# One decoder layer on one Trainium2 core: three weight tiles instead of four beside the time mixing, its tiles in two pools, and nine modulation steps at the second norm

## The chip, the cores and the metric

One core of one Trainium2 chip runs the whole kernel as one launch. The metric is the device time of that launch in microseconds. The chip has five engines that matter here: TensorE (PE, with its weight loads shown apart as PEld), VectorE (DVE), ScalarE (ACT), GpSimd (POOL) and SyncE (SP), which here only issues DMAs.

## The reference

One inference step of one layer on 256 prompt tokens and 8 sequences of 4 sample tokens, so 288 columns (NT) of width 2048, in float32. Cut to what matters:

```python
mod = silu(c) @ ada_w + ada_b                 # 2048 -> 6 vectors of 2048
sh1, sc1, ga1, sh2, sc2, ga2 = split(mod, 6)
h = rmsnorm(x, g0) * (1 + sc1) + sh1
proj = h @ w_in                               # 2048 x 6144: r, k, v and three conv inputs
w, a, g = small low-rank products of h
y, S = wkv7_scan(state, r, w, k, v, kk, kk*a) # 16 heads of 64, delta rule, token by token
o_rwkv = (groupnorm(y) + bonus) * g
o_conv = bg * causal_conv3(cg * hc)
x = x + ga1 * (concat(o_rwkv, o_conv) @ w_out)
h2 = rmsnorm(x, g1) * (1 + sc2) + sh2
ua, ub = split(causal_conv3(h2 @ ffn_up), 2)  # 2048 x 11264
x = x + ga2 * ((silu(ua) * ub) @ ffn_down)    # 5632 x 2048
return rmsnorm(x, final_g), and the new states
```

## The kernel before

Activations lie with the features on the partitions and the 288 columns in the free dimension. Every large product runs in three passes over a reduced float format: `load_piece` (L168) brings a piece of 1 MB of weights into a tile of the ring `rawtile` (L137); `split` (L149) makes of each half of it a rounded copy `whi` (ACT, the cast of L154) and a remainder `wlo` (DVE, L156) in a buffer of the pool `hl`; `mm3` (L163) issues three matmuls of 288 columns for each 128x128 block (`actH`x`whi`, `actL`x`whi`, `actH`x`wlo`, L164 to L166). A half piece is 24 matmuls. The ring has 3 tiles that stay for the whole kernel and some more that `work_pools` (L96) opens for a part: 2 in the first part, 1 beside the decay products and the conv, 0 in the second part, 1 from the output projection on. `hl` has 3 buffers.

The six modulation vectors come from `ada_vector` (L247), a generator whose every step loads 1 MB of `ada_w` into a ring tile and issues four side by side matmuls into a bank named `ada` (printed at L298 and L301, the lines of the helper that issues them). Sixteen steps make a vector. The generator `rest` has the 64 steps of GA1, SC2, SH2 and GA2; each `step(rest)` in the program puts one step among other work, and PE order is chosen by a scheduler that goes by the order of the program, by what is ready and by pools.

The stages, in the order of the span:

- 0 to 42 us set-up and first norm, 42 to 270 us the first three blocks of `w_in` and the low-rank products.
- 270 to 415 us the conv stage. For each of the 8 pairs of heads p: `first(p)`, `blocks_of(p-1)` (64x64 and 32x32 matmuls at L635 and L637 whose results go out as `dN` and `dNs`, L641 and L642), two pieces of the conv's `w_in`, two modulation steps (L725). A period takes 17 us. SP issues the four loads and the small stores in one queue, and a load that waits for its tile holds up whatever stands behind it.
- 415 to 475 us: `substitute` (L644 to L669) inverts 32x32 triangles on DVE and POOL (L664, L665), ACT copies the result (`TL`, L666) and stores it as `dT` and `dTT`, while TensorE drains the rest of the conv.
- 475 to 698 us: `second(p)` eight times, some 25 to 30 us each, chains of small matmuls with DVE and ACT between them. `T1` and `TTc` come back from `dT` and `dTT` through SP (L994 to L998). Three modulation steps stand ahead of it, five behind each p, seven behind the last (L1003). Its tiles lie in one pool, `tm2`.
- 700 to 805 us: the output projection `w_out` through `gemm2` (L1063), 8 double columns with the upper half of the inputs first, so that the conv's half starts it. `turn_out` (L1085) transposes rows of states that go out.
- 805 to 817 us: `taps` (transposes of the conv state of the feed forward, L1044), three modulation steps, the sum over partitions by a matmul with ones (L1120), `rms_scale` (L1025 to L1031, a Newton step on DVE behind exp and ln on ACT), then `make_h2` (L1128 to L1132).
- 817 to 1640 us: `up(g)` and `down(g)` for 11 groups of 4 blocks of the feed forward; then the last norm and the rows `yo` that go out.

## Time and profile before

| | us |
|---|---|
| median of 3 runs | 1698.98 (1683.72 to 1699.15) |
| the profiled execution | 1694.01 |
| its span | 1692.2 |
| mean granted clock of TensorE | 0.983 of full speed |
| PE busy | 1630.8 |
| DVE busy | 1160.7 |
| ACT busy | 713.6 |
| POOL busy | 387.1 |

The page counts busy time in the span; the profiled execution's own time is 1.8 us longer than its span. A row of the timeline ends in a bracket where the engine was idle ahead of it: the idle time, and what released it. `xcount` merges neighbouring instructions. In the view by stretches the column of PEclk is the granted clock of TensorE, 1.00 for 2.4 GHz and 0.5 for 1.2 GHz, so a value between them is a stretch with both. Lines (L154) are lines of the kernel before; in the kernel after the change the same statement has another number.

### The profile page before, as it was taken

The page shows a single profiled execution, that of the slowest core. Times are in us where ns is not written, and L with a number is a line of the kernel's source. Part 1 is how long each engine was busy: PE and PEld are TensorE (multiplying, and loading weights), DVE is VectorE, ACT ScalarE, POOL GpSimd, SP SyncE. Part 2 cuts the span into 40 slices and gives each one's busy share as a digit, 9 for nine tenths or more (in the row PEclk, how much of TensorE's full clock was granted, in tenths as well). Part 3 has the DMA queues.
Part 4 walks back from the last instruction along what each step waited for, and adds up shares of the span by engine and source line. Part 5 has one row for each costly group of instructions (what it writes and reads, how often), then busy time and mean ns, then how long its engine had stood idle before and what let it go on. Part 6 is the DMA issues. An engine that isn't in the chain of part 4 may idle for free.

```text
span 1692.2 us, 32395 instructions
## 1 busy us (share of the span) xinstructions
PE 1630.8 (96%) x12713; PEld 1481.5 (88%) x12713; DVE 1160.7 (69%) x2464; ACT 713.6 (42%) x1281; POOL 387.1 (23%) x853
## 2 busy tenths in 40 slices
PE   6999999999889999899899999999999999999996
PEld 3778898889866666699799999999999999999996
DVE  3687798977846665554776676757676766757586
ACT  4543355444234433333654343443434343434444
POOL 2132011221633232100143031221213131221212
PEclk9999999999979999999999999999999999999998
DMA  8897865688567667954654545545545445445532
GB/s 274 287 334 270 281 214 191 198 254 258 160 181 248 215 232 247 331 175 141 224 175 150 175 157 168 174 152 173 163 162 174 151 150 183 166 156 169 174 125 76
DMA packets 238306, 333.61 MB, mean 197 GB/s; under 512 B 35698, under 2 KB 180826, under 8 KB 229546
## 3 DMA queue, kind: packets, MB, share of 16 engines
q1 hardware_dynamic: 234937, 324.55, 58.8%
q0 software_dynamic: 2848, 6.20, 1.1%
q8 instruction: 100, 1.64, 0.4%
q10 hardware_dynamic: 368, 0.79, 0.2%
q14 instruction: 53, 0.43, 0.1%
HBM read 321.63 MB, written 9.89 MB: 196 GB/s over the span
## 4 chain that ended last, share of the span: by engine, by line
PE 84%; DVE 8%; ACT 3%; DMA 2%; POOL 1%; issue 1%; SPq 0%; DVEq 0%; ACTq 0%
PE acc L164 22%; PE acc L166 22%; PE acc L165 22%; PE ada L298 5%; DVE wlo L156 2%; PE acc L298 2%; ACT whi L154 1%; PE wb L298 1%; PE wa L298 1%; PE acc L301 1%; PE wa L301 1%; PE ada L301 1%; DMA A<-in_x_sample_dram 1%; PE wb L164 1%; PE wb L166 0%
## 5 line engine op out<-in xcount | busy, mean ns | idle before, releaser
L164 PE MATMUL acc<-actH,whi 128*128 128x288 f32 (+1 forms) x2368 | 707.1, 299 | 9.0 <-ACT whi L154 5.2
L165 PE MATMUL acc<-actL,whi 128*128 128x288 f32 (+1 forms) x2368 | 703.6, 297 | 0.1
L166 PE MATMUL acc<-actH,wlo 128*128 128x288 f32 (+1 forms) x2368 | 700.9, 297 | 2.8 <-DVE wlo L156 2.7
L156 DVE TENSOR_TENSOR wlo<-raw,whi 128x1024 fp32r<-128x1024 f32 (+1 forms) x391 | 478.6, 1226 | 217.3 <-ACT whi L154 211.0
L154 ACT CAST whi<-raw 128x1024 fp32r<-128x1024 f32 x400 | 417.6, 1048 | 475.9 <-PE acc L165 409.3
L164 PEld LDWEIGHTS acc<-actH,whi 128*128 128x128 f32 x2368 | 448.6, 189 | 20.2 <-ACT whi L154 9.7
L166 PEld LDWEIGHTS acc<-actH,wlo 128*128 128x128 f32 x2368 | 447.8, 190 | 5.6 <-DVE wlo L156 4.6
L165 PEld LDWEIGHTS acc<-actL,whi 128*128 128x128 f32 x2368 | 448.3, 189 | 0.4 <-DVE actL L161 0.3
L164 PE MATMUL acc<-gH,whi 128*128 128x288 f32 x704 | 209.1, 297 | 1.7 <-DVE rd L1051 1.7
L166 PE MATMUL acc<-gH,wlo 128*128 128x288 f32 x704 | 210.4, 299 | 0.0
L165 PE MATMUL acc<-gL,whi 128*128 128x288 f32 x704 | 205.7, 292 | 0.0
L1144 POOL COPY uO<-ub 128x2 f32<-128x2 f32 x88 | 24.6, 280 | 548.6 <-ACT ub L1142 548.6
L164 PEld LDWEIGHTS acc<-gH,whi 128*128 128x128 f32 x704 | 132.3, 188 | 3.8 <-PE acc L166 3.7
L165 PEld LDWEIGHTS acc<-gL,whi 128*128 128x128 f32 x704 | 134.0, 190 | 0.0
L166 PEld LDWEIGHTS acc<-gH,wlo 128*128 128x128 f32 x704 | 132.0, 187 | 0.7
L1049 DVE SCALAR_TENSOR_TENSOR xT<-acc,modT,xT 128x256 f32<-128x256 f32 x192 | 91.7, 477 | 27.6 <-PE acc L166 27.6
L301 PE MATMUL ada<-raw,cT 128*32 128x512 f32 x576 | 109.3, 623 | 0.0
L298 PE MATMUL ada<-raw,cT 128*32 128x512 f32 x192 | 100.0, 623 | 1.0 <-DMA raw<-in_ada_w_dram 0.7
L1149 DVE SCALAR_TENSOR_TENSOR uz<-ub,cw,uz 128x304 f32<-128x304 f32 x176 | 96.5, 548 | 4.3
L1141 POOL COPY ub<-sF 128x16 f32<-128x16 f32 x88 | 71.2, 809 | 103.9 <-ACT sF L1045 103.9
L1147 DVE TENSOR_SCALAR uz<-ub,cw 128x304 f32<-128x304 f32 x88 | 33.1, 376 | 49.5 <-ACT ub L1143 49.5
L463 DVE TENSOR_TENSOR A<-acc,A 128x296 f32<-128x296 f32 x96 | 44.2, 463 | 29.0 <-PE acc L166 28.5
(449 smaller groups left out, 1985.0 us busy)
## 6 DMA issues: line engine op xcount, KB each, us to landing
raw<-in_ada_w_dram SPq DMA_DIRECT2D x88, 1024.0 KB, 5.2
raw<-in_ffn_up_dram SPq DMA_DIRECT2D x88, 1024.0 KB, 5.1
raw<-in_w_in_dram SPq DMA_DIRECT2D x48, 1024.0 KB, 7.4
raw<-in_ffn_down_dram SPq DMA_DIRECT2D x44, 1024.0 KB, 5.2
raw<-in_w_out_dram SPq DMA_DIRECT2D x16, 1024.0 KB, 5.9
raw<-in_ada_w_dram SPq DMA_DIRECT2D x16, 512.0 KB, 8.0
dX<-xT SPq DMA_DIRECT2D x1, 2304.0 KB, 16.0
xT<-dX POOLq DMA_DIRECT2D x4, 576.0 KB, 9.3
```

The source lines that it names most:

```text
L154: S.copy(hi, raw)
L156: (GP if cur['share'] and cur['turns'] % cur['share'] == 0 else V).tensor_tensor(lo, raw, hi.bitcast(F32), SUB)
L164: E.matmul(acc, wh, xh, start=start, stop=False)
L165: E.matmul(acc, wh, xl, start=False, stop=False)
L166: E.matmul(acc, wl, xh, start=False, stop=stop)
L298: ins = calls[0]().ins
L301: c()
L463: V.tensor_tensor(A[:, t, 2:LW], acc[:, :NL], A[:, t, 2:LW], ADD)
L1049: V.scalar_tensor_tensor(xT[:, t, :T0], acc[:, :T0], modT[:, m, t, 0:1], xT[:, t, :T0], MUL, ADD)
L1141: GP.tensor_copy(bv[:, :, 0:2], sF[:, :, j].rearrange("p (b t) -> p b t", t=2))
L1147: V.tensor_scalar(z[:, :NC - 2], b[:, 0:NC - 2], cw[:, 0, j:j + 1], None, MUL)
L1149: V.scalar_tensor_tensor(z[:, :NC - 2], b[:, t:NC - 2 + t], cw[:, t, j:j + 1], z[:, :NC - 2], MUL, ADD)
```

## The change

What it does, part by part:

1. The conv stage has 3 ring tiles instead of 4 (`work_pools(0)`). The space goes to a pool `inv` that opens already there and holds `T1` and `TTc`, into which the second part loads the inverted triangles; `tc_` and `sp_` move to a longer lived pool too.
2. The tiles of the second part lie in two pools: `tm2` (what ends early) and `tm2q` on the other side (`S0w`, `UVe`, `w2h`, `w2l`, needed to the end). The row tile `so` is now `UVe[0]`.
3. The pool `hl` of the part from `w_out` on is split into one of 1 buffer and one of 2, which take turns 2, 2, 1; the single one lies in space that `tm2q` had before.
4. Modulation steps: 5 behind p = 0 to 5, 3 behind p = 6, 1 behind p = 7 (before 5 and 7), so 8 fewer there. At the second norm 9 instead of 3, with the loads of the first two pieces of `ffn_up` issued between the fifth and the sixth; the last 2 of the 64 run in the feed forward's first group.
5. `rows`, a tile of 3 x 2048, serves as three more ring tiles from `w_out` to the last but one group, then as the result rows `yo`. The ring has 7 tiles there instead of 4.
6. `w_out`'s second double column uses other banks (`wa`), `taps` runs inside `w_out`, behind its fifth double column, and `rms_scale` has three DVE operations behind exp instead of four.

The arithmetic of the products is the same. The diff, cut to its core:

```diff
         if products:
-            cur['hl'] = st.enter_context(pool("hlp", 3, side="right"))
+            cur['hl'] = [st.enter_context(pool(f"hl{n}", n, side="right")) for n in ((1, 2) if apart else (3,))]
...
     def rawtile():
-        cur['turn'] = (cur['turn'] + 1) % (3 + cur['more'])
+        n = 3 + cur['more']
+        cur['turn'] = (cur['turn'] + 1) % (n + len(cur['spare']))
+        if cur['turn'] >= n:
+            return cur['spare'][cur['turn'] - n]
...
+        hl = cur['hl'][0 if cur['turns'] % 3 == 2 else -1]
...
         work.close()
-        work = work_pools(1)
+        invx = ExitStack()
+        inv = invx.enter_context(pool("inv", side="right"))
+        T1, TTc = (inv.tile([P, NP * 4, 32], F32, name=name) for name in ("T1", "TTc"))
+        work = work_pools(0)
...
-        with pool("tm2", 2) as wp:
+        with pool("tm2q", side="right") as wq, pool("tm2") as wp:
...
+            S0w = one(wq, "S0w", NB, CL)
+            UVe = [one(wq, f"UVe{n}", NB, CL) for n in range(2)]
+            w2h, w2l = one(wq, "w2h", 2, P, dtype=F32R), one(wq, "w2l", 2, P, dtype=F32R)
...
-                so = wp.tile([P, NB // 2, P], F32, tag="UVe", name="so")
+                so = UVe[0].rearrange("p b i -> p (b i)").rearrange("p (b x) -> p b x", x=P)
...
-                for _ in range(5 if p < NP - 1 else 7):
+                for _ in range((5, 3, 1)[max(p - NP + 3, 0)]):
                     step(rest)
...
-        fctx.enter_context(work_pools(1))
+        invx.close()
+        fctx.enter_context(work_pools(1, apart=True))
+        cur['turn'], cur['turns'] = -1, 0
...
-            V.tensor_tensor(t, rs, rs, MUL)
-            V.tensor_tensor(t, t, v, MUL)
-            V.tensor_scalar(t, t, -0.5, 1.5, MUL, ADD)
-            V.tensor_tensor(rs, rs, t, MUL)
+            V.scalar_tensor_tensor(v, v, -0.5, rs, MUL, MUL)
+            V.tensor_tensor(v, v, rs, MUL)
+            V.scalar_tensor_tensor(rs, v, 1.5, rs, ADD, MUL)
...
+        rows = fp.tile([P, 3, D], F32, name="rows")
+        cur['spare'] = [rows[:, n] for n in range(3)]
...
-            gemm2(i['w_out'][0], [(256 * c2, ev)], (1, 0))
-            if c2 in ():
-                step(rest)
+            gemm2(i['w_out'][0], [(256 * c2, ev)], (1, 0), ("wa",) if c2 == 1 else ("acc",))
+            if c2 == 4:
+                taps()
         rest_until(48)
-        taps()
-        for _ in range(3):
-            step(rest)
...
+        for _ in range(5):
+            step(rest)
+        loaded = [load_piece(i['ffn_up'][0], 0, 8, c0, 256) for c0 in (0, F)]
+        for _ in range(4):
+            step(rest)
         rs = rms_scale(ps)
```

Where instructions stand now. The queue of SP in the conv stage, one period of the kernel before: `w_in` and `ada_w` are the loads into ring tiles, `dN` and `dNs` the small stores of `blocks_of`.

```order
L170 DMA raw<-in_w_in_dram 128x8x256 x2
L252 DMA raw<-in_ada_w_dram 128x2048
L642 DMA dN<-ws 128x4x64
L252 DMA raw<-in_ada_w_dram 128x2048
L641 DMA dNs<-ws 32x4 x2
L170 DMA raw<-in_w_in_dram 128x8x256 x2
```

The same queue in the changed kernel:

```order
L257 DMA raw<-in_ada_w_dram 128x2048
L175 DMA raw<-in_w_in_dram 128x8x256 x2
L652 DMA dN<-ws 128x4x64
L651 DMA dNs<-ws 32x4 x2
L257 DMA raw<-in_ada_w_dram 128x2048 x2
```

The two stores stood behind the four loads or among the last two; now they stand between the two pieces of `w_in` and the two loads of `ada_w`, and these loads cannot be issued before the stores' own waits are over.

ACT's queue at the end of the conv stage and the start of the second part, before: `TL` is printed as `ws` at L666, `dTT` and `dT` are the stores behind it, `whi` the casts of the conv's last pieces.

```order
L160 CAST actH<-XA 128x288
L792 COPY ws<-XA 128x288
L154 CAST whi<-raw 128x1024
L160 CAST actH<-ws 128x288 x2
L160 CAST actH<-XA 128x288
L797 COPY ws<-XB 128x32
L797 COPY ws<-A 128x32
L160 CAST actH<-ws 128x288 x4
L666 COPY ws<-ws 64x1024
L669 DMA dTT<-ws 128x1024
L668 DMA dT<-ws 64x1024
```

And in the changed kernel, where the copy of `TL` is L676 and the stores L678 and L679:

```order
L159 CAST whi<-raw 128x1024 x2
L677 DMA dTs<-ws 128x16
L159 CAST whi<-raw 128x1024 x8
L706 COPY ws<-acc 128x288
L159 CAST whi<-raw 128x1024
L676 COPY ws<-ws 64x1024
L679 DMA dTT<-ws 128x1024
L678 DMA dT<-ws 64x1024
L706 COPY ws<-acc 128x288
L159 CAST whi<-raw 128x1024 x4
```

The copy and both stores moved from behind the last cast of weights and seven casts of activations to ahead of the last casts of weights.

PE's queue at the end of the second part, before: `wb<-l1h,w2h` is the gate's product, `acc<-actH,whi` the first matmuls of `w_out`, `shO` and `coO` the rows of states.

```order
L164 MATMUL wb<-l1h,w2h 128x288
L165 MATMUL wb<-l1l,w2h 128x288
L166 MATMUL wb<-l1h,w2l 128x288
L1085 MATMUL wb<-con,shO 16x128
L298 MATMUL ada<-raw,cT 32x512
L301 MATMUL ada<-raw,cT 32x512 x3
L298 MATMUL ada<-raw,cT 32x512
L301 MATMUL ada<-raw,cT 32x512 x3
L1085 MATMUL wb<-con,coO 16x128
L164 MATMUL acc<-actH,whi 128x288
L165 MATMUL acc<-actL,whi 128x288
L164 MATMUL acc<-actH,whi 128x288
```

And in the changed kernel, where `con,S0w` are the transposes of the states and `wb<-actH,conr` the group norm's sums, which came well ahead of `w_out` before:

```order
L170 MATMUL acc<-actL,whi 128x288
L171 MATMUL acc<-actH,wlo 128x288 x2
L169 MATMUL acc<-actH,whi 128x288
L170 MATMUL acc<-actL,whi 128x288
L171 MATMUL acc<-actH,wlo 128x288
L960 MATMUL wb<-con,S0w 128x128 x4
L782 MATMUL wb<-actH,conr 128x288
L783 MATMUL wb<-actL,conr 128x288
L169 MATMUL acc<-actH,whi 128x288
```

The first matmuls of `w_out` now stand among the last steps of `second(7)`, with no modulation step between them, instead of behind its end.

## Rows read from the trace of the kernel before

**Rows 1.** The page: PE's busy share, and the chain that ended last.

```profile
PE 1630.8 (96%) x12713; PEld 1481.5 (88%) x12713; DVE 1160.7 (69%) x2464; ACT 713.6 (42%) x1281; POOL 387.1 (23%) x853
...
PE 84%; DVE 8%; ACT 3%; DMA 2%; POOL 1%; issue 1%; SPq 0%; DVEq 0%; ACTq 0%
```

**Rows 2.** Busy time by stretch; last columns: granted clock, DMA share, GB/s.

```profile
core 0: us, PE busy (x) PEld busy (x) DVE busy (x) ACT busy (x) POOL busy (x), PEclk, DMA share, GB/s
374.00:391.00 17.00, 17.00 (x136) 14.80 (x135) 12.81 (x27) 8.10 (x15) 4.60 (x8) 1.00 0.93 300
431.00:456.00 25.00, 23.87 (x179) 23.43 (x177) 23.05 (x43) 8.50 (x10) 21.86 (x41) 1.00 0.58 188
460.00:475.00 15.00, 15.00 (x92) 14.88 (x92) 12.22 (x43) 5.62 (x13) 4.42 (x17) 0.80 0.40 140
475.00:490.90 15.90, 11.95 (x146) 8.24 (x145) 5.92 (x25) 8.55 (x24) 7.35 (x24) 0.76 0.91 163
490.90:504.00 13.10, 13.10 (x96) 9.77 (x96) 5.71 (x14) 2.20 (x6) 2.44 (x9) 0.51 0.61 230
672.00:698.00 26.00, 22.18 (x209) 11.49 (x209) 16.56 (x42) 5.93 (x16) 6.62 (x10) 1.00 0.89 312
698.00:705.00 7.00, 5.24 (x21) 4.95 (x21) 4.04 (x4) 3.71 (x8) 4.65 (x11) 0.51 1.03 341
804.00:817.00 13.00, 7.31 (x60) 4.07 (x58) 8.22 (x26) 6.52 (x15) 2.12 (x4) 0.89 0.86 279
817.00:824.00 7.00, 7.00 (x38) 6.82 (x39) 7.00 (x20) 5.96 (x13) 3.07 (x2) 0.71 0.80 247
```

**Rows 3.** Timeline of PE, 440 to 491 us: idle ahead, and its releaser.

```profile
443.10 0.53 PE L166 MATMUL acc<-actH,wlo 128*128 128x288 f32 x2 [1.13 <-DVE wlo L156]
...
459.88 0.58 PE L164 MATMUL acc<-actH,whi 128*128 128x288 f32 x1 [3.80 <-DVE ws L703]
...
487.17 0.60 PE L301 MATMUL acc<-T,ws 32*32 32x32 f32 x8 [2.73 <-DMA T<-dT]
```

**Rows 4.** Groups of DVE, 430.5 to 474.4 us, the substitution.

```profile
L156 DVE TENSOR_TENSOR wlo<-raw,whi 128x1024 fp32r<-128x1024 f32 x10 | 13.3, 1334 | 2.0 <-ACT whi L154 2.0
L665 DVE TENSOR_TENSOR ws<-ws 128x3 f32<-128x3 f32 (+31 forms) x34 | 11.5, 338 | 0.7
L664 DVE TENSOR_TENSOR ws<-ws 128x3 f32<-128x3 f32 (+31 forms) x34 | 11.3, 332 | 0.7
```

**Rows 5.** The chain that ended last: one modulation step, and single matmuls of 288 columns.

```profile
680.93 0.98 PE ada L301 x4
...
804.18 0.13 PE acc L164
```

**Rows 6.** The chain that ended last, 474 to 489 us: start, us, what.

```profile
474.36 2.06 ACT ws L666
...
476.44 4.21 DMA dT<-ws
...
483.57 5.46 DMA TTc<-dTT
```

**Rows 7.** Timeline of PE, 697 to 700 us.

```profile
697.73 0.28 PE L1085 MATMUL wb<-con,coO 128*16 128x128 f32 x1 [2.57 <-DVE A L986]
699.77 0.61 PE L164 MATMUL acc<-actH,whi 128*128 128x288 f32 x1 [1.76 <-ACT whi L154]
```

**Rows 8.** Timeline of PE, 816 to 817 us.

```profile
816.85 0.85 PE L164 MATMUL wa<-actH,whi 128*128 128x288 f32 x2 [4.28 <-ACT actH L160]
```

**Rows 9.** Timeline of ACT, 814 to 815 us.

```profile
814.43 1.04 ACT L154 CAST whi<-raw 128x1024 fp32r<-128x1024 f32 x1 [2.58 <-DMA raw<-in_ffn_up_dram]
```

**Rows 10.** Timeline of DVE, 811 to 812 us.

```profile
811.41 0.46 DVE L1029 TENSOR_TENSOR rms_t<-rms_t,rms_v 128x288 f32<-128x288 f32 x1
```

**Rows 11.** DMA issues, 306 to 415 us: KB each, median us to landing.

```profile
raw<-in_w_in_dram SPq DMA_DIRECT2D x13, 1024.0 KB, 7.1
raw<-in_ada_w_dram SPq DMA_DIRECT2D x12, 1024.0 KB, 5.1
```

More of the change, by code (lines that the diff above doesn't have):

```diff
@@ L94, with work_pools @@
     psp = ctx.enter_context(pool("psp", 1, PSUM))
-    def work_pools(more, products=True):
+    def work_pools(more, products=True, apart=False):
         st = ExitStack()
@@ L151, in split @@
         n = raw.shape[2]
-        hi = cur['hl'].tile([P, 1024], F32R, tag="whi", name="whi")[:, :k * n].rearrange("p (k n) -> p k n", n=n)
-        lo = cur['hl'].tile([P, 1024], F32R, tag="wlo", name="wlo")[:, :k * n].rearrange("p (k n) -> p k n", n=n)
+        hl = cur['hl'][0 if cur['turns'] % 3 == 2 else -1]
+        hi = hl.tile([P, 1024], F32R, tag="whi", name="whi")[:, :k * n].rearrange("p (k n) -> p k n", n=n)
+        lo = hl.tile([P, 1024], F32R, tag="wlo", name="wlo")[:, :k * n].rearrange("p (k n) -> p k n", n=n)
         S.copy(hi, raw)
@@ L511 @@
         pend = Bp.tile([P, NP, 12], F32, name="pend")
+        tc_, sp_ = Bp.tile([P, NP, TS], F32, name="tc"), Bp.tile([P, CL], F32, name="sp")
         dN = dr.tile([NP, 4, P, CL], F32, name="dN")
@@ L582, in lora2 @@
                 for n, dst, b in ((0, XA, w0v), (1, XB, a0v)):
-                    hi = cur['hl'].tile([P, 1024], F32R, tag="whi", name="whi")
-                    lo = cur['hl'].tile([P, 1024], F32R, tag="wlo", name="wlo")
+                    hi = cur['hl'][0].tile([P, 1024], F32R, tag="whi", name="whi")
+                    lo = cur['hl'][0].tile([P, 1024], F32R, tag="wlo", name="wlo")
                     split_act(hi[:96], lo[:96], raw[:96, n])
@@ L735 @@
         work = work_pools(0, False)
-        with pool("tm2", 2) as wp:
-            def twice(shape, name):
-                return [wp.tile(shape, F32, name=f"{name}{n}", bufs=1) for n in range(2)]
+        with pool("tm2q", side="right") as wq, pool("tm2") as wp:
             (AR0, BK0, AM0, vp, BKh, AR1, BK1, AM1), off = views(
@@ L762, in loads @@
                     return None
-                s0r = wp.tile([P, NB // 2, P], F32, tag="s0r", name="s0r")
+                s0r = s0b[p % 2]
                 for h in range(2):
@@ L818, in second @@
                 St = [None, Cbd[:, 0], k[:, 0:P], k[:, P:2 * P], S4]
-                AX = wp.tile([P, 4, 2, CL], F32, tag="AX", name="AX", bufs=1)
                 BKt, UV = BKtr(), UVr()
@@ L941, in second @@
                 E.transpose(ps[:, :P], S4, ident)
-                sp_ = wp.tile([P, CL], F32, tag="sp", name="sp", bufs=1)
                 for h in range(2):
@@ L946, in second @@
                 ps = bk("wb")
-                UVe = [wp.tile([P, NB, CL], F32, tag="UVe", name="UVe") for _ in range(2)]
                 for h in range(2):
@@ L979, in second @@
                 V.tensor_tensor(y, y, bon, ADD)
-                w2h = wp.tile([P, 2, P], F32R, tag="w2h", name="w2h", bufs=1)
-                w2l = wp.tile([P, 2, P], F32R, tag="w2l", name="w2l", bufs=1)
                 split_act(w2h, w2l, w2)
@@ L1171, in up @@
                 if j2 == 0:
-                    gemm2(i['ffn_up'][0], [a, b], tags=("wa", "wb"), pre=make_h2)
+                    gemm2(i['ffn_up'][0], [a, b], tags=("wa", "wb"), pre=make_h2, loaded=loaded)
                 else:
@@ L1230 @@
             if g == NG - 1:
-                yo += [fp.tile([P, 2, D], F32, name="yoP"), fp.tile([32, D], F32, name="yoS")]
+                yo += [rows[:, 0:2], rows[:32, 2]]
                 tc.keep_in_program_order(S.preload_act_table_set('natural_log_exp_and_others'))
```

23 lines of the change are left out of this document (12 added, 11 removed).

## The prediction

> **What bounds the kernel now.** The page comes first: TensorE is busy for 96% of the span, and the chain that ended last runs through it for 84% [rows 1]. So the change can only win back what TensorE loses: idle time, and time at the lower of its two clocks. It does not touch the amount of matmul work. Second I read the view by stretches [rows 2]. In each row the idle time is the stretch minus PE busy, and the clock's loss is PE busy times (1 minus PEclk). A conv period (374 to 391) has none of either: 17.00 of 17 us at 1.00. The losses lie in four places, all of which the change touches:
>
> - A, the drain of the conv beside the substitution (431 to 475): idle 25.00 - 23.87 = 1.1 and a wait of 3.8 at its end, clock 15.0 x 0.20 = 3.0, together 7.9 us.
> - B, the start of the second part (475 to 504): idle 15.90 - 11.95 = 3.95, clock 11.95 x 0.24 = 2.9 and 13.10 x 0.49 = 6.4, together 13.2. The clock's share is an upper bound, since much there is short matmuls whose time does not follow the clock alone.
> - C, the end of the second part (672 to 705): idle 3.82 + 1.76 = 5.6, clock 5.24 x 0.49 = 2.6, together 8.2.
> - D, the second norm (804 to 824): idle 13.00 - 7.31 = 5.7, clock 7.00 x 0.29 = 2.0, together 7.7.
>
> That is 37 us in all, the most that the change could win. Third comes PE's timeline, whose brackets name the releasers [rows 3]: a wait of 1.13 us for DVE's `wlo`, one of 3.80 for DVE's evacuation of the conv, one of 2.73 for the load of the inverted triangles. After 3.80 the clock is 1.2 GHz; after 1.13 it is not [rows 2, 3].
>
> **The change part by part.** Modulation steps, transposes and products are only moved, so their PE time cancels: what counts is which of the 37 us goes, and what new loss comes.
>
> *A.* DVE is busy 23.05 of 25 us in the drain [rows 2]: 11.5 + 11.3 = 22.8 us of substitution and ten `wlo` of 1.33 us [rows 4]. The last `blocks_of` now stands one pair of modulation steps and 96 matmuls earlier on TensorE: 2 x 0.98 + 96 x 0.133 (eight of these matmuls on the chain take 1.06 us; one is shown) [rows 5] = 14.7 us more product time behind which the same DVE work lies. That covers the 4.9 us of stalls on paper. But DVE takes its work in order, and eight `wlo` still stand among the substitution's rows, so a stall of a kind like 1.13 may stay or come earlier. I take 3.5 of 7.9, with ends of 8 gained and 3 lost (one more stall of the size of the 3.80).
>
> *B.* Before, the copy of `TL` (2.06), the store `dT` (4.21) and the load of `TTc` (5.46) follow each other on the chain at the start of the second part [rows 6]. ACT's copy now stands ahead of the conv's last casts, and the pool that holds `T1` and `TTc` is open, so the loads can land while the drain still runs. The wait of 2.73 goes, and 0.3 beside it; late next is the rest of the 3.95, short waits on DVE and POOL of some 0.4 us each, which stay. The copy delays the casts behind it by 2.06 us, hidden by casts that run one buffer ahead of TensorE; uncovered it would cost 2.1. The clock stays low there because one wait follows another; with the longest gone I take half of a lower 7 us. So 3.0 + 3.5 = 6.5, ends 0 and 13.
>
> *C.* Before, `w_out` begins after the last step of `second(7)`, behind waits of 2.57 and 1.76 us [rows 7], the latter for a cast that waited for a buffer. The eight modulation steps that stood there (8 x 0.98 = 7.8 us [rows 5]) were filler of a chain that set its own length; now the first `w_out` matmuls are the filler, the eight go elsewhere. I leave 2.4 of the 5.6 idle (the half piece whose buffer lies in the late pool waits for the states' stores) and count the clock's 2.6 as gone: 5.8, ends 2 and 8.
>
> *D.* Six more modulation steps, 5.9 us, fill 5.7 of holes. The hole that they cannot fill is the last, 4.28 [rows 8]. Its chain was a `whi` cast that waited 2.58 for the first piece of `ffn_up` [rows 9], then the first `h`. With three more ring tiles that piece is loaded early, worth 1.1 where `h` becomes late next, and one DVE operation of 0.46 is gone [rows 10]: about 2.7 remains. Whether 2.7 us of idle lowers the clock no row here settles (2.73 came while it was already low); I count the 2.0 as gone. So 3.0 + 2.0 = 5.0, ends 2 and 8.
>
> *The ring of three.* Four loads a period of 17 us share three tiles instead of four. A tile's turn may take 3/4 x 17 = 12.75 us on average. A conv piece takes 7.1 to land [rows 11], 2 x 1.04 for its casts [rows 9] and 1.33 for the last `wlo` [rows 4], 10.5; a modulation step 5.1 [rows 11] + 0.98, 6.1; mean 8.3, so 4.5 us of slack. What eats into it: the casts wait for `hl`, and in SP's queue the stores of `blocks_of`, which wait for DVE and ACT, now stand ahead of the two modulation loads and the next piece. I take +2.0 us; ends 0 and +24 (eight periods of 3.0: three loads issued together behind one store, at the 300 GB/s of the period [rows 2] 3 x 3.5 = 10.5 us for the third, of which one piece's product, 48 x 0.133 = 6.4, and one step, 0.98, cover 7.4).
>
> By the Trainium skill, page "DMA: Bandwidth & Descriptors", section "Anatomy of one DMA", a DMA takes about 2 us plus its bytes at 436 GB/s (told for GpSimd's path; these go through SP), an estimate of 4.4 us for 1 MB; the turns would be 7.8 and 5.4, the +2.0 would be 0 and the sum 2 us lower. The measured 7.1 and 5.1 are longer because loads overlap, so I keep the rows.
>
> Sum against the profiled execution: -3.5 - 6.5 - 5.8 - 5.0 + 2.0 = -18.8, or 1694.0 - 18.8 = 1675.2. The median shown lies 5.0 above that execution, so the forecast is 1680.
>
> **The rivals.**
>
> *Only the waits go.* The clock still falls at B, C and D, because waits of some 2 to 3 us remain, and A's stalls only move. Then B gives 3.0, C 3.2, D 3.0, the ring costs 2.0: -7.2, or 1692. For it: in B TensorE stays at 0.51 in the stretch 490.9 to 504 although it was busy all the time [rows 2]. Against it: 504 to 672 and the conv period show full clock with small gaps.
>
> *The ring starves the conv stage.* Each of eight periods waits some 3.0 us for its third load and restarts at the lower clock as after the 3.80, 3.0 each: 48 instead of the 2.0, so -20.8 + 48 = +27, or 1726. It decides from 20.8 / 8 = 2.6 us per period. For it: DMA share 0.93 in the period [rows 2], and the stores ahead of the loads. Against: the 4.5 us of slack. The Trainium skill speaks for the second half of it: page "TensorE: Matmul & The Clock Gate", section "HAM oscillation — how this bites in real kernels", has the clock fall anew in every wait for a load between groups of matmuls; the trace shows that for one wait, the 3.80, and no wait of the conv stage here tests it.
>
> *The late buffers hold `w_out`.* The change doesn't do what it says at C: the third and fourth half pieces wait for the stores of `second(7)`, TensorE has no modulation steps to fill the chain, and C gives 2.0 instead of 5.8: -15.0, or 1684.
>
> *All of it comes.* A gives 7.9, B 10, C and D 10.8, the ring costs nothing: -28.7, or 1670.
>
> **How the numbers follow.** Forecast 0.40, only the waits 0.30, all of it 0.14, late buffers 0.06, starved ring 0.10. A measurement of this kernel tells about 1% from no change, 17 us: under 1682 is faster, over 1716 slower. The forecast lies just on the faster side, so 0.24 of its 0.40 counts there, with the 0.14 of "all of it" and 0.07 from "only the waits" and "late buffers": 0.45. Slower gets most of the starved ring, 0.09; the rest, 0.46, is within 1%. The range runs from 1662, past "all of it", to 1701, past the case without the clock; outside are the starved ring and tails. The likeliest case alone has 1672 to 1688.
>
> **What would show it.** In the changed trace: conv periods of 17.0 to 17.5 us with PE full and clock 1.00 (over 19 is the starved ring); no wait for `T<-dT` and a clock above 0.8 in the first 25 us of the second part; `w_out` matmuls that begin right behind the `UVe` products and no clock step at their start; a hole of 2 to 3 us ahead of the first `h2` matmul, at full clock after it. The prediction is wrong if the conv stage grows by over 8 us, if the clock stretches at B, C and D remain, or if TensorE's idle time in A to D stays above 15 of the 20.2 us.

## The result and the profile after

The changed kernel takes 1704.78 us, median of 20 runs (1695.98 to 1710.51), beside 1694.19 us for the kernel before, measured again in 20 runs. The ratio (of the means) is 1.0052, with an interval of 1.0032 to 1.0072: slower by half a per cent, where 1680 was forecast. The profiled execution took 1697.11 us, the fifth shortest of the 20 and 7.7 under their median, that of the kernel before 0.2 under its own, so one profile shows less of the loss than the median does.

The page of the changed kernel, the busy time of the engines and the chain that ended last, beside [rows 1]:

```profile
PE 1632.5 (96%) x12713; PEld 1484.5 (88%) x12713; DVE 1161.2 (68%) x2463; ACT 713.6 (42%) x1281; POOL 378.1 (22%) x853
...
PE 82%; DVE 10%; ACT 3%; DMA 2%; issue 1%; POOL 1%; SPq 0%; DVEq 0%; ACTq 0%
```

TensorE is busy for 1.7 us more than before, with the same 12713 matmuls, and the span is 1695.3 us, 3.1 longer. But the set-up was 3.7 us shorter in this execution (the first large product starts at 34.5 instead of 38.2 us). That is chance: over all 14 profiled executions of this study it starts between 34.1 and 40.5, in kernels that do not differ there. From that product on the changed kernel is 6.8 us longer, beside 0.0052 x 1694 = 8.8 us by the ratio (5.4 to 12.2 by its interval).

To see where, I cut the span at events that both kernels have: the first and the last matmuls of `blocks_of`, the last conv product, the transposes of the states in `second(0)` and in `second(5)`, the first `w_out` matmul, the sum with ones, the first `up` matmul, the last `down` matmul. The view by stretches of the changed kernel, one row for each stretch (the stretch from `second(0)` to `second(5)` is 130.3 us in both and left out, and the first part, 257.2 and 258.0):

```profile
core 0: us, PE busy (x) PEld busy (x) DVE busy (x) ACT busy (x) POOL busy (x), PEclk, DMA share, GB/s
292.54:404.72 112.18, 108.58 (x844) 94.38 (x844) 90.91 (x198) 47.15 (x85) 26.32 (x51) 0.97 0.72 228
404.72:483.92 79.20, 71.98 (x502) 69.17 (x502) 59.34 (x134) 26.92 (x36) 29.53 (x72) 0.94 0.71 207
483.92:514.82 30.90, 29.13 (x312) 19.51 (x310) 17.40 (x55) 12.68 (x40) 12.04 (x40) 0.83 0.63 205
645.14:693.66 48.52, 44.14 (x444) 29.34 (x441) 28.06 (x74) 16.56 (x47) 9.21 (x13) 0.90 0.57 188
693.66:807.03 113.37, 111.87 (x831) 108.16 (x829) 62.41 (x109) 44.94 (x63) 7.47 (x17) 0.98 0.65 210
807.03:814.32 7.29, 4.21 (x28) 1.17 (x28) 4.88 (x15) 3.01 (x7) 1.96 (x2) 0.93 0.99 412
814.32:1680.29 865.97, 862.46 (x6437) 850.57 (x6438) 594.47 (x1163) 367.91 (x604) 196.75 (x453) 1.00 0.50 163
```

And the same stretches in the kernel before:

```profile
295.39:414.93 119.54, 119.54 (x952) 104.35 (x952) 99.57 (x210) 53.21 (x92) 29.34 (x54) 1.00 0.74 235
414.93:474.82 59.89, 54.97 (x391) 54.31 (x390) 49.50 (x124) 19.01 (x28) 30.16 (x71) 0.94 0.55 168
474.82:511.34 36.52, 32.18 (x313) 21.54 (x311) 16.96 (x55) 14.24 (x41) 11.22 (x39) 0.72 0.76 205
641.68:699.77 58.09, 52.45 (x526) 30.83 (x523) 32.71 (x86) 18.68 (x56) 12.54 (x19) 0.99 0.78 268
699.77:808.20 108.43, 108.43 (x803) 106.31 (x804) 55.29 (x94) 40.37 (x52) 4.44 (x12) 0.98 0.62 193
808.20:816.85 8.65, 2.96 (x21) 1.25 (x17) 6.24 (x19) 3.89 (x8) 1.75 (x2) 0.85 1.03 348
816.85:1677.15 860.30, 855.91 (x6393) 849.50 (x6394) 596.94 (x1162) 369.47 (x605) 202.27 (x453) 1.00 0.49 160
```

The reader is to take two numbers from each row: the stretch minus PE busy is idle time, and PE busy times (1 minus PEclk) is what the lower clock cost, at most. PEclk is a mean over the whole stretch, idle time included, and rounded; the table counts TensorE's busy time inside the 1.2 GHz stretches and halves it.

| stretch | before: us, idle, clock | after: us, idle, clock | difference |
|---|---|---|---|
| conv periods | 119.5, 0.0, 0.0 | 112.2, 3.6, 3.0 | with the drain |
| drain and substitution | 59.9, 4.9, 3.1 | 79.2, 7.2, 4.9 | +12.0 |
| start of the second part | 36.5, 4.3, 8.7 | 30.9, 1.8, 5.1 | -5.6 |
| `second(5)` to `w_out` | 58.1, 5.6, 0.0 | 48.5, 4.4, 3.9 | -9.6 |
| `w_out` | 108.4, 0.0, 2.6 | 113.4, 1.5, 1.8 | +4.9 |
| second norm | 8.6, 5.7, 0.0 | 7.3, 3.1, 0.0 | -1.4 |
| feed forward | 860.3, 4.4, 2.1 | 866.0, 3.5, 2.9 | +5.7 |

The last four rows add up to -0.3 us; here the forecast had its terms C and D, together -10.8. The first three add up to +6.3, where it had -8.0 (A, B and the ring).

The waits behind these rows, from PE's timeline in the conv stage (the first two) and in the drain, beside [rows 3]:

```profile
317.10 0.54 PE L171 MATMUL acc<-actH,wlo 128*128 128x288 f32 x2 [1.48 <-DVE wlo L161]
...
349.98 0.61 PE L169 MATMUL acc<-actH,whi 128*128 128x288 f32 x1 [1.93 <-ACT whi L159]
...
434.20 0.70 PE L171 MATMUL acc<-actH,wlo 128*128 128x288 f32 x2 [2.55 <-DVE wlo L161]
...
444.97 0.58 PE L169 MATMUL acc<-actH,whi 128*128 128x288 f32 x1 [2.34 <-DVE ws L722]
```

And at the end of the second part and at the norm, beside [rows 6, 7 and 8]; the first row is the last modulation step in the stretch:

```profile
673.86 0.61 PE L306 MATMUL ada<-raw,cT 128*32 128x512 f32 x3
...
682.25 0.88 PE L306 MATMUL wa<-ws,A 64*64 64x64 f32 x12 [0.58 <-DVE Cb L913]
...
685.28 0.37 PE L303 MATMUL wb<-XB,Cb 128*64 128x64 f32 x1 [1.06 <-DVE XB L923]
...
691.75 1.11 PE L303 MATMUL wb<-UVe,ws 128*64 128x512 f32 x1 [0.51 <-ACT sp L950]
...
814.32 0.85 PE L169 MATMUL wa<-actH,whi 128*128 128x288 f32 x2 [3.08 <-ACT actH L165]
```

Of the two waits ahead of `w_out` in [rows 7], of 2.57 and 1.76 us, nothing is left, and the last hole of the norm is 3.08 instead of 4.28. But between 674 and 692 us there is not one modulation step any more, and a row of new waits of 0.4 to 1.1 us stands in its place.

### The profile page after: what moved, and what is told of

The parts are those of the page before. It is cut to its first block, busy times and chain, and to the rows that moved or that the text cites. A ratio compares the mean times of both kernels' runs of the same rounds, so it can differ in the third digit from the quotient of the medians.

```text
span 1695.3 us, 32411 instructions
## 1 busy us (share of the span) xinstructions
PE 1632.5 (96%) x12713; PEld 1484.5 (88%) x12713; DVE 1161.2 (68%) x2463; ACT 713.6 (42%) x1281; POOL 378.1 (22%) x853
## 4 chain that ended last, share of the span: by engine, by line
PE 82%; DVE 10%; ACT 3%; DMA 2%; issue 1%; POOL 1%; SPq 0%; DVEq 0%; ACTq 0%
PE acc L169 22%; PE acc L171 21%; PE acc L170 21%; PE ada L303 4%; DVE wlo L161 2%; PE acc L303 2%; ACT whi L159 1%; PE wb L303 1%; PE acc L306 1%; PE wa L303 1%; PE wa L306 1%; PE wb L169 1%; DMA A<-in_x_sample_dram 1%; PE wa L170 1%; PE wb L171 1%
## 5 line engine op out<-in xcount | busy, mean ns | idle before, releaser
L169 PE MATMUL acc<-actH,whi 128*128 128x288 f32 (+1 forms) x2336 | 700.0, 300 | 8.0 <-ACT whi L159 5.6
L171 PE MATMUL acc<-actH,wlo 128*128 128x288 f32 (+1 forms) x2336 | 693.0, 298 | 7.2 <-DVE wlo L161 6.9
L170 PE MATMUL acc<-actL,whi 128*128 128x288 f32 (+1 forms) x2336 | 695.5, 298 | 0.1
L159 ACT CAST whi<-raw 128x1024 fp32r<-128x1024 f32 (+1 forms) x294 | 306.2, 1047 | 354.8 <-PE acc L170 282.6
L161 DVE TENSOR_TENSOR wlo<-raw,whi 128x1024 fp32r<-128x1024 f32 (+1 forms) x285 | 347.7, 1223 | 155.3 <-ACT whi L159 149.2
L171 PEld LDWEIGHTS acc<-actH,wlo 128*128 128x128 f32 x2336 | 442.7, 190 | 11.5 <-DVE wlo L161 10.3
L161 DVE TENSOR_TENSOR wlo<-rows,whi 128x1024 fp32r<-128x1024 f32 x106 | 129.5, 1222 | 67.0 <-ACT whi L159 64.9
L159 ACT CAST whi<-rows 128x1024 fp32r<-128x1024 f32 x106 | 111.4, 1051 | 125.8 <-PE acc L170 121.7
L306 PE MATMUL ada<-raw,cT 128*32 128x512 f32 x534 | 98.0, 607 | 0.0
L303 PE MATMUL ada<-raw,cT 128*32 128x512 f32 x178 | 89.8, 607 | 0.3 <-DVE modT L296 0.3
```

The costliest lines, as they stand in the source:

```text
L159: S.copy(hi, raw)
L161: (GP if cur['share'] and cur['turns'] % cur['share'] == 0 else V).tensor_tensor(lo, raw, hi.bitcast(F32), SUB)
L169: E.matmul(acc, wh, xh, start=start, stop=False)
L170: E.matmul(acc, wh, xl, start=False, stop=False)
L171: E.matmul(acc, wl, xh, start=False, stop=stop)
L303: ins = calls[0]().ins
```

## The experiments

Each experiment was compared with runs of the kernel before on the same chip. Two sums serve as measures besides the ratio: the end part, from the states' transposes of `second(5)` to the end of the span (1050.6 us before, 1050.2 in the changed kernel), and the front part, from the first blocks to the transposes of `second(0)` (216.0 before, 222.3 changed).

**ring3_only: the kernel before with three tiles.**

```diff
-        work = work_pools(1)
+        work = work_pools(0)
```

> The kernel before with nothing changed but the conv stage's ring, 3 tiles instead of 4 (the freed 8 KB stay empty). Theory 1 (the ring is the cause): from the first blocks to the last conv product the time grows by 8 to 12 us as in the changed kernel (idle there about 10.8 instead of 4.9, more time at the lower clock), the second part starts with the same wait for the triangles' loads as before, the rest is as before: total +8 to +12 us, ratio 1.005 to 1.007. Theory 2 (the early loads into the new pool are the cause, by what they push back in SP's queue): this stretch stays within 2 us of before, ratio 1.000 +- 0.001.

Measured: ratio 1.0081 (1.0056 to 1.0105). The view by stretches, for the conv periods, the drain, the start of the second part, and a piece further on:

```profile
291.81:404.38 112.57, 108.83 (x844) 94.64 (x844) 91.44 (x199) 47.01 (x85) 26.85 (x51) 0.97 0.72 226
404.38:483.73 79.35, 72.13 (x503) 69.33 (x502) 59.34 (x134) 26.88 (x36) 29.83 (x72) 0.94 0.65 200
483.73:515.04 31.31, 28.59 (x312) 19.17 (x310) 17.52 (x55) 12.63 (x40) 12.03 (x40) 0.84 0.79 219
632.00:653.00 21.00, 20.89 (x128) 10.18 (x126) 7.50 (x24) 3.55 (x11) 1.52 (x6) 0.51 0.41 121
```

The first two rows are 191.9 us long where before has 179.4: +12.5, a little over the 8 to 12 of theory 1 (as the ratio is over its 1.005 to 1.007), and the drain's idle time is the same 7.2 us as in the changed kernel. So the ring alone makes the loss. But the third row was missed by the expectation: it is 31.3 instead of 36.5 us although the triangles' tiles are in their old place. The giving back comes with the ring too. (The last row is for the section on the hardware; what that stretch lost at the lower clock is in this execution and not in the changed kernel's.)

**inv_only: the three tiles and the new pool.**

```diff
-        work = work_pools(1)
+        invx = ExitStack()
+        inv = invx.enter_context(pool("inv", side="right"))
+        T1, TTc = (inv.tile([P, NP * 4, 32], F32, name=name) for name in ("T1", "TTc"))
+        work = work_pools(0)
...
```

> The kernel before with the ring of 3 and the new pool for the inverted triangles; everything from the second part's tiles on as before. Theory 1: the ring's +8 to +12 less the 6 us that the start of the second part gives: +2 to +6 us, ratio 1.001 to 1.004. Theory 2: the same total, but ring3_only would be near 1.000, so the pair tells them apart.

Measured: ratio 1.0089 (1.0067 to 1.0112); front part 223.1 us, ring3_only 223.2. The start of the second part is 30.8 beside 31.3 us. The pool brings half a microsecond at most; the expected 1.001 to 1.004, and with it the difference between the pair, was missed. Theory 2 had already fallen with ring3_only, which it put at 1.000.

**cd_only: everything else of the change, with the ring of 4.**

```diff
-        invx = ExitStack()
-        inv = invx.enter_context(pool("inv", side="right"))
-        T1, TTc = (inv.tile([P, NP * 4, 32], F32, name=name) for name in ("T1", "TTc"))
-        work = work_pools(0)
+        work = work_pools(1)
...
+            T1, TTc = one(wp, "T1", NP * 4, 32), one(wp, "TTc", NP * 4, 32)
```

> The changed kernel with the conv stage's ring and the triangles' tiles as before (4 tiles, loads behind the second part's pools). Theory 1: conv stage and drain as before (idle 4.9, 119.5 and 59.9 us long), the start of the second part as before, and from p = 5 of the second part to the first product of the feed forward no gain, as in the changed kernel (within 1.5 us of the 175.2 us plus five modulation steps that run later): total -1 to +3 us, ratio 0.999 to 1.002. Forecast's terms (C and D give 10.8): -10 us, ratio 0.994.

Measured: ratio 1.0016 (0.9992 to 1.0040), end part 1051.2 us, conv periods and drain 119.5 and 59.9 as before. So the ring is all of the loss at the front, and the rest of the change is worth nothing as it stands. Two stretches of it, the start of the second part and `second(5)` to `w_out`:

```profile
475.37:515.15 39.78, 37.03 (x313) 24.04 (x311) 17.41 (x55) 14.32 (x41) 12.16 (x41) 0.61 0.72 200
645.47:699.61 54.14, 48.24 (x458) 32.76 (x456) 29.56 (x77) 18.11 (x51) 11.71 (x17) 0.87 0.48 152
```

The first has TensorE's instructions in the same order as before, yet 39.8 instead of 36.5 us: less idle time (2.8 instead of 4.3 us), and 14.7 instead of 8.7 us lost to the clock. The second has 5.9 us idle and a clock of 0.87.

**steps_back: the changed kernel with the old distribution of modulation steps.**

```diff
-                for _ in range((5, 3, 1)[max(p - NP + 3, 0)]):
+                for _ in range(5 if p < NP - 1 else 7):
...
-        for _ in range(5):
+        for _ in range(3):
             step(rest)
         loaded = [load_piece(i['ffn_up'][0], 0, 8, c0, 256) for c0 in (0, F)]
-        for _ in range(4):
-            step(rest)
```

> The changed kernel with the old distribution of the modulation steps (5 behind each p, 7 behind the last, 3 at the second norm, whose first pieces of ffn_up are still loaded early). Theory 3 (the steps taken out of the last two p had filled holes and kept the clock up): no stretch at the lower clock before the output projection, idle there as small as before, so 3 to 6 us better than the changed kernel, ratio 0.999 to 1.002 to before. Rival (the steps were on the path and the pools are what holds the end): no better than the changed kernel, ratio 1.004 to 1.007.

Measured: ratio 1.0067 (1.0042 to 1.0091), end part 1050.8 us. Theory 3's number was missed, and the rival's 1.004 to 1.007 was met. Theory 3's mechanism held in one half: no time at the lower clock ahead of `w_out`, where the changed kernel loses 3.9 us. But with all seven steps behind the last p the stretch is 58.6 us long again, idle 6.75, and the norm idles 5.5. Neither seven steps nor one is right; the next has four.

**steps_mid: cd_only with the steps halfway.**

```diff
-                for _ in range((5, 3, 1)[max(p - NP + 3, 0)]):
+                for _ in range(5 if p < NP - 1 else 4):
...
-        for _ in range(5):
+        for _ in range(3):
             step(rest)
         loaded = [load_piece(i['ffn_up'][0], 0, 8, c0, 256) for c0 in (0, F)]
-        for _ in range(4):
+        for _ in range(3):
             step(rest)
```

> cd_only with the modulation steps halfway: 5 behind each p, 4 behind the last, 6 at the second norm (3, the loads of ffn_up, 3). If steps behind the last p keep TensorE's clock up: from p = 5 to the first product of the feed forward no more than 2.7 us lost at the lower clock (cd_only 7.0, before 2.6) and idle 8 to 9.5 (cd_only 10.1, before 11.3), so 3 to 5 us less lost than in cd_only, ratio 0.997 to 1.000. If only idle time counts: within 1.5 us of cd_only.

Measured: 1681.24 us, ratio 0.9926 (0.9900 to 0.9952), the only kernel of the study that is clearly faster than both (of the others only mid_early's interval ends below 1, at 0.9997), and better than either case had said (0.997 to 1.000 by the first). End part 1040.2 us, 10.4 of the 12.5 us that the ratio stands for. Its stretches from `second(5)` on; the start of the second part was 32.2 us:

```profile
640.74:689.41 48.67, 47.35 (x489) 28.78 (x487) 28.62 (x75) 15.94 (x47) 9.45 (x13) 1.00 0.76 254
689.41:798.89 109.48, 109.09 (x825) 105.74 (x823) 62.00 (x108) 45.40 (x63) 7.50 (x17) 1.00 0.75 235
798.89:806.17 7.28, 4.89 (x36) 1.59 (x32) 4.87 (x15) 3.49 (x8) 1.97 (x2) 1.00 1.01 358
806.17:1665.66 859.49, 854.73 (x6394) 847.72 (x6394) 594.60 (x1164) 367.63 (x603) 201.01 (x453) 1.00 0.49 159
```

The reader is to compare the first row with the fourth row of the changed kernel: 48.67 and 48.52 us, the same length, with PE busy for 47.35 instead of 44.14 us at full instead of 0.90 of the clock. It holds eleven modulation steps where the changed kernel holds six. The five more steps cost nothing there; in the changed kernel they run in the feed forward, whose stretch is 866.0 instead of 859.5 us. The largest wait left at the end of the second part:

```profile
688.65 0.66 PE L958 MATMUL wb<-con,S0w 128*128 128x128 f32 x4 [0.87 <-DVE S0w L954]
```

**after_mid: the same steps in the changed kernel, ring of 3.** The edit is that of steps_mid.

> The changed kernel with the modulation steps halfway (5 behind each p, 4 behind the last, 3 + 3 at the second norm) and all else as changed, the ring of 3 too. If the steps behind the last two p are what the changed kernel lacked at its end: 8 to 11 us better than it between p = 5 and the end, total ratio to before 0.998 to 1.001, with the 12 us of the ring's conv stage and the 5 us back at the start of the second part unchanged. If the gain of steps_mid needs the ring of 4: ratio 1.003 to 1.006.

Measured: ratio 1.0002 (0.9975 to 1.0029), end part 1041.1 us (changed 1050.2), front part 222.9. As the first case said: the two causes are apart, and they add. Its rows for `second(5)` to `w_out`, `w_out`, and the feed forward:

```profile
651.35:700.01 48.66, 47.35 (x489) 28.78 (x487) 28.63 (x75) 15.92 (x47) 9.45 (x13) 1.00 0.75 255
700.01:810.73 110.72, 109.47 (x826) 105.88 (x824) 62.19 (x108) 45.51 (x63) 7.50 (x17) 1.00 0.72 232
818.02:1677.27 859.25, 855.40 (x6394) 849.05 (x6394) 594.78 (x1163) 367.96 (x603) 199.80 (x453) 1.00 0.49 159
```

**steps_51: steps_mid with five steps behind p = 6, one behind the last.**

```diff
-                for _ in range(5 if p < NP - 1 else 4):
+                for _ in range(5 if p < NP - 1 else 1):
```

and 5 + 4 at the norm.

> steps_mid with 5 steps behind p = 6, 1 behind the last and 9 at the norm (5 + 4). If TensorE needs the steps inside the last p's chain: idle there of 3 us or more and a stretch at the lower clock before or in the output projection, no or little gain over cd_only (ratio 0.998 to 1.002). If it was the three steps behind p = 6 that mattered: as steps_mid, ratio 0.991 to 0.996.

Measured: ratio 0.9982 (0.9957 to 1.0007), end part 1047.6. The stretch from `second(5)` to `w_out`:

```profile
648.56:702.88 54.32, 50.30 (x474) 32.85 (x471) 29.39 (x77) 18.41 (x51) 11.94 (x17) 0.86 0.58 190
```

Idle 4.0 us and a clock of 0.86, as the first case said: it is the steps inside the last p that TensorE lacks. The other three ran in the feed forward, whose stretch is 862.2 us, beside 859.5 in steps_mid.

**late3: four tiles in the conv periods, three in the drain.** The triangles' tile is the ring's fourth tile until the last blocks are issued.

```diff
+        tri = inv.tile([P, 2048], F32, name="tri")
...
+        work = work_pools(0)
+        cur['spare'] = [tri]
...
+            cur['spare'] = []
             blocks_of(NP - 1)
             substitute()
```

> The kernel before with the triangles' tile serving as the ring's fourth tile until the last blocks are issued, 3 tiles only for the drain, and the early loads. Starvation (the conv stage loses because its fourth tile is gone): the eight periods are as before, no idle from the first blocks to the last; what the drain loses with 3 tiles and 22 substitution rows in a row on DVE shows alone: 2 to 6 us more than before's 59.9 for the same products, and up to 6 us given back at the start of the second part, total -3 to +3 us, ratio 0.998 to 1.002. Rival (the loss is all in the drain's order): total as inv_only, +6 to +10.

Measured: ratio 1.0029 (1.0006 to 1.0052). Conv periods, drain, start of the second part:

```profile
295.67:415.27 119.60, 119.60 (x951) 104.39 (x952) 99.11 (x212) 52.16 (x91) 29.62 (x55) 1.00 0.71 226
415.27:479.54 64.27, 56.57 (x391) 55.80 (x390) 52.08 (x123) 21.29 (x29) 28.44 (x68) 0.92 0.65 188
479.54:518.49 38.95, 36.67 (x312) 23.67 (x310) 17.74 (x55) 12.87 (x40) 11.96 (x40) 0.65 0.61 178
```

With four tiles the conv periods have no idle time: starvation is shown. The drain is 4.4 us longer than before (7.7 idle), with 22 rows of substitution between two `wlo` on DVE. The expected giving back at the start of the second part did not come (38.95 us), so the total lies just above the 0.998 to 1.002 that was said.

**ring3_hl4: three tiles, four buffers for the halves.**

```diff
-        work = work_pools(1)
+        work = work_pools(0, 4)
```

where the second number is now that of the buffers of `hl`.

> ring3_only with the freed 8 KB as a fourth buffer for the rounded weights and their remainders, which lets a tile be split sooner and TensorE run one half piece (3.2 us) further while DVE is busy with the substitution. If tiles held too long by waiting splits and DVE's order are what starves TensorE: 6 us or more of ring3_only's 12.5 us between the first blocks and the end of the conv go, total ratio 1.001 to 1.004. If the three tiles themselves (loads issued too late) are: within 3 us of ring3_only there, ratio 1.005 to 1.009.

Measured: ratio 1.0077 (1.0044 to 1.0111); conv periods and drain 191.0 us, ring3_only 191.9. One more buffer gives 0.9 us at most (the five other kernels with three tiles and the blocks early have 191.4 to 192.3): it is not the split halves that hold the tiles.

**ring3_stores: three tiles, the small stores on POOL's queue.**

```diff
-        work = work_pools(1)
+        work = work_pools(0)
...
-                    nc.sync.dma_start(dNs[h, p], nr[S32])
-                nc.sync.dma_start(dN[p].rearrange("c s t -> s c t"), nt)
+                    GP.dma_start(dNs[h, p], nr[S32])
+                GP.dma_start(dN[p].rearrange("c s t -> s c t"), nt)
```

> ring3_only with the small stores dN and dNs issued by POOL's queue instead of SP's, so that no load of weights stands behind a store; their order on SP is again two conv pieces, two modulation loads. If the queue (stores ahead of loads) is what starves the conv stage with 3 tiles: no idle from the first blocks to the last (ring3_only 3.7, and 3.3 lost at the lower clock). If the three tiles are: idle of 2.5 us or more there, as in ring3_only. The drain has 20 substitution rows between two wlo either way and loses 2 to 5 us against before. Total ratio 1.000 to 1.004 by the queue, 1.005 to 1.009 by the tiles.

Measured: ratio 1.0113 (1.0075 to 1.0151). Conv periods and drain:

```profile
297.56:423.61 126.05, 122.80 (x956) 106.54 (x956) 98.88 (x211) 52.14 (x91) 43.37 (x76) 0.99 0.67 233
423.61:490.26 66.65, 56.81 (x391) 55.19 (x390) 52.99 (x124) 21.37 (x30) 31.05 (x71) 0.92 0.59 177
```

In this kernel the blocks stand where they stood before, so the first row compares with before's 119.54 directly: 126.05, idle 3.25. The stores' place in SyncE's queue is not the cause; with three tiles the conv's loads wait for modulation steps here too (SP's waits for them: 42.7 us in 8 times). But POOL is busy 14 us more in the periods, 12.9 of it with issuing the stores, and the ratio is above the expected 1.005 to 1.009, so not all of the 6.5 us need be the tiles'. The drain is 66.65 us with 9.8 idle.

**early_sub: the last blocks early, ring of 4.**

```diff
                 if p:
                     blocks_of(p - 1)
+                if p == NP - 1:
+                    blocks_of(p)
...
-            blocks_of(NP - 1)
             substitute()
```

> The kernel before with the last pair's blocks (and so the substitution's inputs) issued ahead of the last two conv pieces of the loop; ring of 4. Theory (the 5 us given back at the start of the second part in the changed kernel come from the earlier substitution, not from the new pool): the start of the second part 30.5 to 32 us long instead of 36.5, at 4 tiles and with T1 and TTc in their old place; the drain pays 0 to 4 us for 20 substitution rows between two wlo: total -5 to 0 us, ratio 0.997 to 1.000. Rival (the pool brings it): 36 us there, total 0 to +4.

Measured: ratio 0.9994 (0.9968 to 1.0021). The drain and the start of the second part, and the one wait that makes up the drain's idle time, from PE's timeline:

```profile
414.93:486.71 71.78, 62.82 (x451) 60.68 (x451) 53.67 (x131) 25.02 (x35) 30.03 (x72) 0.93 0.59 169
486.71:516.21 29.50, 27.53 (x313) 18.15 (x311) 17.29 (x55) 12.53 (x40) 11.16 (x39) 0.88 0.78 228
```

```profile
446.26 0.85 PE L166 MATMUL acc<-actH,wlo 128*128 128x288 f32 x2 [8.92 <-DVE wlo L156]
```

The start of the second part is 29.5 us, without the new pool: the earlier substitution brings that. And one wait of 8.92 us for a `wlo` takes as much in the drain.

**mid_early: steps_mid and early_sub together.** Both edits as above.

> steps_mid with the last pair's blocks ahead of the last two conv pieces, as in early_sub, ring of 4. early_sub moved 6 us from the start of the second part into the drain and gained nothing clear; if that adds to steps_mid: ratio 0.990 to 0.994, no different from steps_mid beyond its interval.

Measured: 1692.28 us, ratio 0.9976 (0.9955 to 0.9997); end part 1039.7 us as in steps_mid, start of the second part 39.3 us with 14.9 lost to the clock. The expected 0.990 to 0.994 was missed; what early_sub won at the start of the second part did not come again.

## Why the prediction was wrong

Two of the prediction's own signs of being wrong came: the conv stage with its drain grew by 12.0 us, over the 8, and stretches at the lower clock remained at B, C and D.

**The ring of three** was put at +2.0 us, with ends of 0 and +24, and with A at -1.5; the two stretches of both grew by 12.0 us, and by 12.5 in ring3_only. No other place failed by as much (C and D together by 10.5). What failed is the sentence "a modulation step 5.1 [rows 11] + 0.98, 6.1; mean 8.3, so 4.5 us of slack". The step's tile is not free 0.98 us after it lands: it is held until TensorE reaches the step in its order. In the changed kernel the load of one step was issued at 291.99 and landed at 296.9, and TensorE reached the first of the two steps that were then loaded at 307.05:

```profile
291.99 0.34 SPq L257 DMA_DIRECT2D raw<-in_ada_w_dram  x1
...
307.05 0.62 PE L303 MATMUL ada<-raw,cT 128*32 128x512 f32 x1
```

That is a turn of 16 us instead of 6.1. SyncE's waits in the conv stage of the changed kernel show what it does to the loads behind it (columns: us in total, times, longest):

```profile
SPq L175 <- PE ada L306: 39.8, 6, 7.9
```

Before, with four tiles, the same wait was the first of these rows; the second is that of the modulation loads, which in the changed kernel do not wait for such a matmul:

```profile
SPq L170 <- PE ada L301: 7.9, 1, 7.9
SPq L252 <- PE ada L301: 15.0, 3, 5.7
```

So before the waits of this kind were spread, 22.9 us in all; with three tiles they are 39.8 and fall on the conv's second pieces, six times. One of these was issued behind the step at 308, landed at 313.4, and ACT's cast waited for it:

```profile
313.46 2.11 ACT L159 CAST whi<-raw 128x1024 fp32r<-128x1024 f32 x2 [0.21 <-DMA raw<-in_w_in_dram]
```

`wlo` followed it behind other DVE work, and TensorE stood still for 1.48 us at 317.10. An average turn with slack says nothing when the turns are tied to each other's order. With the blocks in their old place the three tiles cost at most 6.5 us in the periods (ring3_stores). For the whole front part, after what is given back, the ring's cost is 222.9 us (mean of five executions with 3 tiles: the changed kernel, ring3_only, inv_only, steps_back, after_mid) less 216.9 (mean of four with 4: before, cd_only, steps_mid, steps_51; they lie between 211.8 and 220.5), 6.0 us. By the ratios it is more: some 13 to 15 us in ring3_only, inv_only and ring3_hl4 and in after_mid beside steps_mid, 6 only in the changed kernel beside cd_only. The last section has 8.7 us that two of these profiles lose elsewhere; where the rest lies stays open.

**A, the drain,** was put at -3.5; its idle time grew from 4.9 to 7.2 us and its clock's loss from 3.1 to 4.9. The earlier start was there, but the sentence "That covers the 4.9 us of stalls on paper" failed. The cover is product time on TensorE, but the products need a `wlo` every 3.2 us from the same DVE, and the program put ten pairs of rows without one there. Between the last `wlo` ahead and the next, DVE's timeline of the changed kernel:

```profile
423.46 1.21 DVE L161 TENSOR_TENSOR wlo<-raw,whi 128x1024 fp32r<-128x1024 f32 x1
...
432.26 0.48 DVE L675 TENSOR_TENSOR ws<-ws 128x192 f32<-128x192 f32 x1
432.67 1.48 DVE L161 TENSOR_TENSOR wlo<-raw,whi 128x1024 fp32r<-128x1024 f32 x1
```

From 424.6 to 432.7 us DVE did nothing but substitution, and TensorE waited 2.55 us for that `wlo`. early_sub shows it in its pure form, with four tiles: 8.92 us.

**B, the start of the second part,** was put at -6.5 and came out at -5.6, by another way than the text gave. That "the pool that holds `T1` and `TTc` is open" was worth 0.5 us at most (inv_only beside ring3_only). The rest goes with the earlier blocks and substitution: with the blocks early the stretch took 29.5 to 31.4 us in seven of eight executions (ring3_only and ring3_hl4 have no new pool, early_sub not even the three tiles) and 39.3 in the eighth (mid_early); with the blocks in their old place 32.2 to 39.9 in six. The means are 32.0 and 37.8. Within each group the difference is the clock: with nearly the instructions of before this stretch took 36.5, 39.8, 32.2 and 39.9 us in four executions (before, cd_only, steps_mid, steps_51), and between 4.5 and 14.7 us of it went to the clock. "The clock stays low there because one wait follows another" does not fit them: cd_only idles less there than before and loses 6 us more. One execution can't carry a term of 6 us here, and the prediction built one on it; that the number came out so near is in part luck.

**C, the end of the second part,** was put at -5.8. The step that failed is "now the first `w_out` matmuls are the filler". They begin only behind the `UVe` products at 693.7 us, where the prediction itself looked for them; from 675 to 692 nothing filled the chain. That the eight modulation steps "were filler of a chain that set its own length" was right, and this very sentence should have led to the opposite count: work that lies in a chain's holes is free there, and moved to the feed forward it costs its full 0.98 us a step. Five steps ran there (the description of the change had two), +5.7 us. And the clock's 2.6 us, counted as gone, became 3.9 ahead of `w_out` and 1.8 in it. The emptier chain lost the clock in a stretch whose waits are all small:

```profile
675.00:690.00 15.00, 11.18 (x115) 9.09 (x115) 10.77 (x29) 3.20 (x9) 3.50 (x5) 0.79 0.49 157
```

TensorE was idle for 3.8 of these 15 us, no wait was longer than 1.06 us, and the clock fell to 1.2 GHz at 683.6. With eleven steps in the chain (steps_mid, after_mid) it did not fall, with six or eight (cd_only, steps_51) it did. By the Trainium skill, page "TensorE: Matmul & The Clock Gate", section "HAM oscillation — how this bites in real kernels", waits for loads between groups of matmuls bring the clock down. Here it came down among small waits for DVE and ACT; none of the waits of 0.4 us or more in this stretch was for a load.

**D, the norm,** was put at -5.0. The hole of 4.28 became 3.08 instead of 2.7, so the loaded pieces, the early cast and the shorter `rms_scale` together did nearly what was said; idle fell from 5.7 to 3.1. But of the six more modulation steps only three ran ahead of that hole, the other three in the feed forward. The clock's 2.0 did not come back (feed forward: 2.9 lost instead of 2.1). The size of the hole alone does not decide it: the feed forward lost nothing behind 1.54 us in steps_mid and behind 3.07 in steps_51, and 1.7 us behind 1.60 in after_mid.

C and D together were put at -10.8. With the steps where their holes are, the same pools, tiles, loads and `rms_scale` give 1040.2 - 1050.6 = -10.4 us (steps_mid) and -9.5 (after_mid). The size of that term was right, and the distribution of the steps was what decided whether it was paid. Nothing here tells the parts of the pools, the seven ring tiles, the early loads and the shorter `rms_scale` from each other; that was not tried.

Of the rivals, "only the waits go" (1692) was nearest in place and sign of its reasons: waits went at C and D and the clock stayed low. "The ring starves the conv stage" was right in its mechanism and too high in its price: two waits in eight periods, not eight, and of the two only the one of 1.93 us was followed by the lower clock (349.1 to 355.9 us), the one of 1.48 was not. The 3.80 that the prediction set beside the page on the clock was no wait for a load; its releaser was DVE [rows 3].

**What came out best:** steps_mid, the change without its ring of three and with 4 instead of 1 steps behind the last p and 5 instead of 3 behind p = 6, at 0.9926 of before.

## What to carry to other kernels

Work that fills the holes of a dependent chain is free where it stands; before moving it, ask whether the place it goes to has holes, and count how much of it the chain still needs to stay filled (here four steps behind the last p were better than one and than seven, the only numbers tried). A ring's slack must be counted along the order in which its tiles are released, not as a mean of their turns: one tile that is held until the busiest engine reaches it stops the loads behind it. And an engine that feeds the bottleneck every few microseconds must not be given a long run of other work in a row, however much cover the bottleneck seems to have.

## What the hardware showed that was not expected

Identical instructions ran at different clocks. The start of the second part took 32.2 to 39.9 us in four executions of nearly the same instructions, the difference being time at 1.2 GHz. In ring3_only TensorE was granted 0.51 from 632 to 653 us while it was busy for 20.89 of 21 us (the last row shown for that kernel); the kernel before, with the same instructions there, had full speed. By busy time that is 10.2 us lost, and the stretch from `second(0)` to `second(5)` is 139.0 us instead of 130.3, 8.7 longer. ring3_hl4 lost as much there, the other kernels nothing; both have three tiles, as seven of the 14 profiled kernels do, too few to say that the ring brings it. ring3_only's waits just ahead were 0.51 and 0.48 us, before's 0.40 and 0.49. What set it off no run here shows.
